# A second pair of projections as seven 2x2 block products per layer, with background steps placed by counted time

## The chip, the cores and the metric

The kernel runs on one core of a Trainium2 chip. The metric is the device time of one execution in microseconds (us), as the median of several runs.

## The reference

Two layers, each of them a pre-norm mixer with a residual, work on x of 256 tokens by 2048 channels, all float32. One wide product gives the inputs of two mixers: `qk`, `v`, `o`, `z_a` of a chunked matrix memory (mLSTM) with eight heads, and `xb`, `z_b` of a gated linear recurrence (RG-LRU). A second product, `w_out`, takes both results back to 2048 channels.

```
u = rms_norm(x, norm_g)
p = u @ w_in
qk, v, o, z_a, ig, fg, xb, z_b = jnp.split(p, SPLIT_AT, axis=-1)
...
h = mlstm_chunkwise(q, k, v, i_pre, log_f)
h = h * jax.nn.sigmoid(o.astype(f32)).reshape(b_, s_, H_A, DV_A)
...
y_a = h.astype(x.dtype) * jax.nn.silu(z_a)
xc = causal_dwconv(xb, lru_conv_w) + lru_conv_b
y_b = rg_lru(xc.astype(f32), w_a, b_a, w_x, b_x, lam).astype(x.dtype) * jax.nn.silu(z_b)
return x + jnp.concatenate([y_a, y_b], axis=-1) @ w_out
```

A last `rms_norm` follows the second layer.

## The kernel before

Each layer is worked off in four groups (0 to 3 in the code, one to four in words) of 512 columns of each of `o`, `qk`, `v`, `xb`, `z` and `zb`. `_sequence` writes the order of the items by hand: the projections of a group, among them the four chunks of `w_out` for the group ahead of it, then the gates. An input projection is four *units* of 1024 KB of weights, and a unit is two *halves*. For a half, `prepare` splits 128x1024 weights into a high part `wH` (ScalarE, a cast) and a low part `wL` (VectorE, a subtraction); TensorE then makes 12 matmuls of 128x512 (`mm_a`, L400): two blocks of the contraction, two halves of the tokens, and three products, high by high, high by low and low by high. Splits stand `AHEAD` = 3 halves ahead of their matmuls, in four buffers each; three buffers `raw` hold units that SP's queue loads.

Everything else (turning to channels, convolutions, scores, gates, scans) is written as generators in the queue `bg`. After a half, `pump` advances them until about `FULL` = 3 us of VectorE work is queued (`st["lag"]`). A generator that has to let time pass yields "wait"; before the change a distance in time is a number of such pumps (`LANDING` = 4, `FAR` = 6, `PACE`). `pump` is called only after plain halves, not after block halves. `require(key)` runs generators until a result is there.

`to_channels` and `swapped` turn a 128x1024 tile from tokens to channels: ScalarE scales it into `tok`, VectorE transposes 32x32 blocks into `blk`, four transfers on SP's queue write `moved` in DRAM, and one on POOL's queue reads it back as `fr`. A later step (`ch<-fr`, `zsg<-fr` or `tok<-fr`) reads `fr`. `ch` is one buffer, shared by the `qk` and `xb` convolutions, the scores `Pt` and `zb`.

One pair of items per layer, `z` of group three and `o` of group four (`PAIR`), is done as a product of 2x2 blocks with seven block products instead of eight: x is cut by 128 tokens and by 1024 channels, the weights by 1024 channels and by the two items' columns. A block product is four *block halves* of 128x1024 weights, each with six matmuls into one PSUM bank `ps_b` (`product`, L1175 to L1177). Products 1 to 4 and 5 to 7 use either x itself or `sums` of its blocks, S1 to S4, that VectorE makes (`block_sums`); on the weights' side plain blocks, or sums that transfers make in DRAM (`weight_sums`): SP copies a block to `w_d`, and accumulating transfers on POOL's queue add others to it. `rawb`, two buffers of 512 KB, holds a block half's weights. Results are added up in `res`. Block halves are spread over the plain halves at the end of the program; the main loop below then emits everything in one order, in which each engine works in its own order.

Of the kernel before, what the change touches and what calls it, by code (L numbers as in the profile page):

```python
# [16 lines left out]
P = 128  # L17
# [11 lines left out]
LANDING = 4  # L29
FAR = 6  # L30
BORDER = 7
BLANKS = 7
PACE = 3, 5
# [9 lines left out]
def _sequence():  # L43


    def units(item):
        return [(item, j) for j in range(_nunits(item))]

    seq = []
    for l in range(DEPTH):  # L50
        for g in range(NG):
            fill = [("out", l, g - 1, c) for c in range(4)] if g > 0 else []
            head = {0: ("o", "qk", "v"), 1: ("qk", "o", "v"), 2: ("qk", "o", "v")}.get(g, ("o", "v", "qk"))
            items = [("in", l, k, g) for k in head]
            at = 2 if g == NG - 1 else 0
            items += fill[0:at] + [("in", l, "xb", g)] + fill[at:4]
            items += [("in", l, "z", g), ("gate", l, g)]
            items.insert(len(items) if g > 0 else -2, ("in", l, "zb", g))
            us = [u for it in items for u in units(it)]
            if l > 0 and g == 0:  # L60
                us[0:8] = [us[i] for i in (0, 4, 1, 5, 2, 6, 3, 7)]
            seq += us
        if l + 1 < DEPTH:
            u = [u for c in range(4) for u in units(("out", l, NG - 1, c))]
            seq += [u[i] for i in (0, 2, 1, 3, 4, 5, 6, 7)]
        else:
            seq += units(("last", l, NG - 1))
    return seq


PAIR = (("z", NG - 2), ("o", NG - 1))


def _blockwise(item):

    return item[0] == "in" and item[2:] in PAIR

# [21 lines left out]
def tile_trunk(ctx, tc, x, xt, par, gw, gb, ws, final_g, out):  # L99
# [30 lines left out]
    st = {"nload": 0, "lag": 0.0, "nprep": 0, "pair": 0, "aux": 0}  # L130
# [165 lines left out]

    def require(key):
        i = 0
        while key not in st:
            i = step(i)  # L300

# [8 lines left out]
    def drain():  # L310
        i = 0
        while bg:
            i = step(i)
# [26 lines left out]
    def load_block(hf):  # L340
        raw = hf["raw"] = wblk.tile([P, 2, 512], F32, tag="rawb", name="rawb")
# [336 lines left out]
    def v_post(l, g, acc):  # L678
        vH = work.tile([P, 2, 2, 258], F32R, tag="sB", name="vH")
# [13 lines left out]
    def qk_post(l, g, acc):  # L693
        bg.append(e_gen(l, g))
        fr = to_channels(l, acc)
        relaxed = 0 < g < NG - 1

        def gen():
            for _ in range(LANDING):
                yield "wait"  # L700
            st["turning"] = True
# [4 lines left out]
            for ct in range(4):  # L706
                conv(ch, qc, ct, O_QKW + 4 * (8 * (ct % 2) + 2 * g + ct // 2), l, None)
                yield 1.45
            if relaxed:
# [17 lines left out]
            while any((k, l, g) not in st for k in ("E", "v", "so")):  # L727
                yield "wait"
            E, em, so, (vH, vL) = st["E", l, g], st["em", l], st["so", l, g], st["v", l, g]
# [21 lines left out]
            tt_(PL, Pt, PH.bitcast(F32), ALU.subtract)  # L751
            yield 1.0
# [36 lines left out]
    def z_post(l, g, acc):  # L789
        require(("hn", l, g))  # L790
        require(("rstd", l))
        rstd = st["rstd", l]
# [10 lines left out]
        def gen():  # L803
# [8 lines left out]
            for _ in range(FAR if g < NG - 1 else LANDING):  # L812
# [6 lines left out]
    def xb_post(l, g, acc):  # L819
        fr = to_channels(l, acc)  # L820

        def gen():
            for _ in range(LANDING):
                yield "wait"
            ch = joined(fr)
            yield 0.3
            xc = work.tile([P, 4, T], F32, tag="c4", name="xc", bufs=2)
            for ct in range(4):
                tix = 4 * g + ct
                conv(ch, xc, ct, O_LW + 4 * tix, l, pars[:, l, O_LB + tix : O_LB + tix + 1])  # L830
                yield 1.45
            while ("scores", l, g) not in st:
# [78 lines left out]
    def zb_post(l, g, acc):  # L911
        ending = (l, g) == (DEPTH - 1, NG - 1)
        fr = to_channels(l, acc, nc.sync if ending else G)

        def gen():
            for _ in range(LANDING - 3 if ending else FAR):
# [3 lines left out]
            while st["turning"]:  # L920
                yield "wait"
            xc, _ = st["xc", l, g]
# [9 lines left out]
            for b in range(2):  # L932
# [3 lines left out]
                yield 0.6  # L936
            if ending:
# [107 lines left out]
    def block_sums(l):  # L1045
# [3 lines left out]
        res = st["res", l] = act.tile([P, 4, 512], F32, tag="res", name="res")  # L1049

        def made(i, key, negated, p, q, pieces=1, after=None):
            to, n = sums[i], 8 // pieces
            for k in range(pieces):
                ks = slice(n * k, n * k + n)
                while after and ("done", l, after, (k + 1) * 4 // pieces - 1) not in st:
# [11 lines left out]
                for f in (difference,  # L1067
# [8 lines left out]
                    if pieces == 1:  # L1076
                        yield "wait"
                        yield "wait"
# [15 lines left out]
        for _ in range(5):  # L1094
            yield "wait"
# [5 lines left out]
    def block_unit(l, r, c, j):  # L1101
        return ws[blocks[("in", l) + PAIR[c], 2 * r + j]]

    wd = [[[dram.tile([P, 2048], F32, name=f"w_d{l}{i}{j}") for j in range(2)] for i in range(2)] for l in range(DEPTH)]

    def weight_sums():

        def moved(l, to, start, r, c, j, h):
            cs = slice(1024 * h, 1024 * h + 1024)
            src = block_unit(l, r, c, j)[:, cs]  # L1110
            while not start and st["n"] - st.get("staged", -9) < 2:
                yield "wait"
            if start:
                order(nc.sync.dma_start(out=wd[l][to][j][:, cs], in_=src), st["ld"])
            else:
                i0 = G.dma_start(out=wd[l][to][j][:, cs], in_=src, accum_op=ALU.add)
                order(i0, st["gq"])
                paced(i0, st["wH"])
            for _ in range(PACE[l]):
                yield "wait"  # L1120

        parts = [(j, h) for j in range(2) for h in range(2)]
        while ("hn", 0, 0) not in st:
            yield "wait"
        for l in range(DEPTH):
            for to, a, b in ((0, (0, 0), (0, 1)), (1, (1, 1), (0, 1))):
                for at in parts:
                    yield from moved(l, to, True, *a, *at)
                    yield from moved(l, to, False, *b, *at)
            for no, a in ((5, (1, 1)), (6, (1, 0))):  # L1130
                for j, h in parts:
                    while ("loaded", l, no, 2 * j + h) not in st:
                        yield "wait"
                    yield from moved(l, 0, False, *a, j, h)

    def block_halves(l):
# [8 lines left out]
        def slot(i):  # L1145
            return st["res", l][:, i]
# [5 lines left out]
        def copied(to):  # L1152
            S.copy(out=slot(to), in_=box["b"])

        def end7():
            add(3, 3)
            g1 = PAIR[1][1]

            def gen():
                while ("lru", l, g1 - 1) not in st:  # L1160
                    yield "wait"
                o_post(l, g1, (slot(2), slot(3)), "neg")
                yield 0
            bg.append(gen())

        def product(A, no, kp, need, end):
            opening = kp == 0 and no in (1, 5, 6)
# [11 lines left out]
            def after():  # L1179
                st["done", l, no, kp] = True  # L1180
                if kp == 3:
                    end()
            need_ = (need, l, kp // 2) if need == "S4" and kp % 2 == 0 else (need, l) if need and kp == 0 else None
            if (no, kp) == (5, 3):
                need_ = ("S2", l)
            return dict(i=kp % 2, mm=f, split=None, paired=False, own=None,
                        before=(lambda: require(need_)) if need_ else None, after=after)

        parts = []
        for no, A, need, end, W in (  # L1190
            (1, plain(0, 0), None, lambda: copied(1), (0, 0)),
            (2, plain(0, 1), None, lambda: copied(0), (1, 0)),
            (5, summed(1), "S1", lambda: add(3, 1), 0),
            (3, summed(1), "S4", lambda: add(2, 1), (1, 1)),
            (6, summed(0), "S2", lambda: add(2, 2), 0),
            (7, summed(1), "S3", end7, 1),
            (4, plain(1, 1), None, lambda: add(1, 1), 0),
        ):
            for kp in range(4):
                src = block_unit(l, *W, kp // 2) if isinstance(W, tuple) else wd[l][W][kp // 2]  # L1200
                hf = product(A, no, kp, need, end)
                hf["from"] = src[:, 1024 * (kp % 2) : 1024 * (kp % 2) + 1024]
                hf["loaded"] = ("loaded", l, no, kp)
                parts.append(hf)
        return parts
# [172 lines left out]
    order_, span = [], {}  # L1378
    for item, j in seq:
        l, what = item[1], item[2:]  # L1380
        if _blockwise(item):
            if what == PAIR[0]:
                span[l] = (span[l][0], len(order_))
            continue
        if (item[0], what) == ("in", ("qk" if l else "o", 1)) and l not in span:
            span[l] = (len(order_), None)
        order_ += [dict(hf, at=(item, j)) for hf in units[item][j]]
    for l in reversed(range(DEPTH)):
        a, b = span[l]
        b += b % 2  # L1390
        order_[b - 1]["then"] = lambda l=l: z_post(l, PAIR[0][1], st["res", l][:, 0:2])
        b -= 6
        parts = block_halves(l)
        gates_ = [n for n, hf in enumerate(order_) if hf.get("at", (("",),))[0][0] == "gate"]
        free = [n for n in range(a, b) if not any(g <= n < g + 8 for g in gates_)]
        for i in reversed(range(len(parts))):
            at = free[(i + 1) * (len(free) - 1) // len(parts)]
            order_[at:at] = [parts[i]]
# [8 lines left out]
    for n, hf in enumerate(order_):  # L1407
# [126 lines left out]
```

## Time and profile before

| | |
|---|---|
| median of three runs | 1483.2 us (1482.11 to 1483.34) |
| the profiled execution's time | 1483.14 us |
| its span, first to last instruction | 1481.3 us |
| granted TensorE clock | 0.998 |
| busy: TensorE, VectorE, ScalarE, GpSimd | 1469.4, 1145.2, 956.4, 108.2 us |
| moved by DMA | 383.43 MB, 259 GB/s in the mean |

PE is TensorE and PEld its weight loads, DVE VectorE, ACT ScalarE, POOL GpSimd, SP the engine whose queue begins most loads. Matmul durations overlap: 390 ns is the mean of one, while they start closer together than that. DMA share is the mean busy share of the core's 16 DMA engines. Most operations of VectorE and ScalarE are issued by one helper and have line L113, so groups are told apart by tile names.

### The profile page before, as it was taken

Reading aid. Unit: us, or ns where it says so; the run is one execution under the profiler, and the core shown is the slowest. Engines: PE = TensorE matmul, PEld = TensorE weight load, DVE = VectorE, ACT = ScalarE, POOL = GpSimd, SP = SyncE. Lnnn points to the kernel's source line nnn. Section 1 sums busy time; section 2 is a strip of 40 time slices with the busy share of each in tenths; the row PEclk is TensorE's granted clock in tenths of the full one; section 3 lists DMA queues with packets and bytes.
Section 4 is the critical chain, followed back from the end, with each engine's and each line's share of the span. In section 5 each row is a group of like instructions: output and inputs, shape, how many; then the busy total and the mean of one; then the engine's idle time right before and its main releaser. Section 6 shows DMA issues by size and latency. Waiting matters only on the chain.

```text
span 1481.3 us, 18779 instructions
## 1 busy us (share of the span) xinstructions
PE 1469.4 (99%) x6782; PEld 1226.8 (83%) x6782; DVE 1145.2 (77%) x1564; ACT 956.4 (65%) x1226; POOL 108.2 (7%) x186
## 2 busy tenths in 40 slices
PE   9999999999999999999999999999999999999997
PEld 7888888888888888788888888888888888888886
DVE  5788888888777676778867889789787776767785
ACT  7666765656665765558565677655667566655675
POOL 0010000100100001000000100000000000010002
PEclk9999999999999999999999999999999999999999
DMA  9866898999978998896786657679799668778783
GB/s 344 323 223 228 264 314 274 291 288 279 313 259 267 281 287 275 270 288 210 279 281 199 234 203 252 235 251 282 234 276 299 214 221 254 250 222 264 238 274 116
DMA packets 104045, 383.43 MB, mean 259 GB/s; under 512 B 11392, under 2 KB 31888, under 8 KB 84496
## 3 DMA queue, kind: packets, MB, share of 16 engines
q1 hardware_dynamic: 87536, 327.41, 63.3%
q0 software_dynamic: 13952, 50.35, 15.6%
q10 hardware_dynamic: 2464, 4.47, 0.8%
q8 instruction: 53, 0.87, 0.2%
q14 instruction: 40, 0.33, 0.1%
HBM read 344.95 MB, written 62.41 MB: 275 GB/s over the span
## 4 chain that ended last, share of the span: by engine, by line
PE 91%; DMA 4%; DVE 2%; ACT 1%; issue 1%; SPq 0%; ACTq 0%; DVEq 0%; POOLq 0%
PE acc L400 78%; PE ps_gt L857 3%; DMA raw<-in_ws_dram 3%; PE ps_b L1175 2%; PE ps_b L1176 2%; PE ps_b L1177 2%; DVE wL L113 1%; PE acc L1273 1%; PE acc L1274 1%; PE acc L1272 1%; DMA xp<-in_xt_dram 1%; DMA pars<-in_par_dram 1%; DMA fr<-moved 0%; PE acc_x L1274 0%; PE acc_x L1273 0%
## 5 line engine op out<-in xcount | busy, mean ns | idle before, releaser
L400 PE MATMUL acc<-wH,x_s 128*128 128x512 f32 x2752 | 860.2, 390 | 0.4 <-ACT wH L113 0.4
L113 DVE TENSOR_TENSOR wL<-raw,wH 128x1024 fp32r<-128x1024 f32 (+1 forms) x500 | 598.2, 1203 | 250.0 <-ACT wH L113 248.1
L113 ACT CAST wH<-raw 128x1024 fp32r<-128x1024 f32 (+1 forms) x500 | 515.1, 1036 | 386.5 <-PE acc L400 307.8
L400 PEld LDWEIGHTS acc<-wH,x_s 128*128 128x128 f32 x2752 | 516.5, 188 | 107.3 <-ACT wH L113 0.8
L400 PE MATMUL acc<-wL,x_s 128*128 128x512 f32 x1376 | 534.3, 389 | 0.0
L400 PEld LDWEIGHTS acc<-wL,x_s 128*128 128x128 f32 x1376 | 258.3, 188 | 52.8
L400 PE MATMUL acc<-wH,ybL 128*128 128x512 f32 x224 | 87.1, 390 | 0.2 <-DVE ybL L964 0.2
L400 PE MATMUL acc<-wH,yaH 128*128 128x512 f32 x224 | 87.2, 389 | 0.0
L400 PE MATMUL acc<-wL,ybH 128*128 128x512 f32 x224 | 87.2, 389 | 0.0
L400 PE MATMUL acc<-wH,ybH 128*128 128x512 f32 x224 | 87.2, 389 | 0.0
L400 PE MATMUL acc<-wH,yaL 128*128 128x512 f32 x224 | 87.2, 389 | 0.0
L400 PE MATMUL acc<-wL,yaH 128*128 128x512 f32 x224 | 87.2, 389 | 0.0
L113 ACT ACT_TABLE_LOAD x61 | 78.3, 1283 | 4.8 <-DVE qc L113 1.4
L113 ACT CAST wH<-rawb 128x1024 fp32r<-128x1024 f32 x56 | 59.0, 1053 | 22.9 <-PE acc L400 10.3
L113 DVE TENSOR_TENSOR wL<-rawb,wH 128x1024 fp32r<-128x1024 f32 x56 | 68.2, 1219 | 3.8 <-ACT wH L113 3.0
L522 POOL DMA_DIRECT2D fr<-moved x34 | 19.0, 559 | 532.7 <-DMA moved<-blk 395.3
L113 DVE STREAM_TRANSPOSE blk<-tok 128x1024 f32<-128x1024 f32 x33 | 40.9, 1240 | 13.3 <-ACT tok L113 13.3
L400 PEld LDWEIGHTS acc<-wH,ybL 128*128 128x128 f32 x224 | 42.0, 188 | 9.3 <-DVE ybL L964 0.6
L400 PEld LDWEIGHTS acc<-wH,yaL 128*128 128x128 f32 x224 | 42.0, 188 | 8.7
L400 PEld LDWEIGHTS acc<-wH,ybH 128*128 128x128 f32 x224 | 42.1, 188 | 8.7
L400 PEld LDWEIGHTS acc<-wL,ybH 128*128 128x128 f32 x224 | 42.0, 188 | 8.6
L400 PEld LDWEIGHTS acc<-wL,yaH 128*128 128x128 f32 x224 | 42.1, 188 | 8.5
(224 smaller groups left out, 1601.5 us busy)
## 6 DMA issues: line engine op xcount, KB each, us to landing
raw<-in_ws_dram SPq DMA_DIRECT2D x152, 1024.0 KB, 6.4
raw<-in_ws_dram SPq DMA_DIRECT2D x190, 512.0 KB, 5.9
fr<-moved POOLq DMA_DIRECT2D x34, 512.0 KB, 6.3
moved<-blk SPq DMA_DIRECT2D x132, 128.0 KB, 2.7
w_d<-in_ws_dram POOLq DMA_DIRECT2D x32, 512.0 KB, 10.0
rawb<-w_d SPq DMA_DIRECT2D x32, 512.0 KB, 6.6
rawb<-in_ws_dram SPq DMA_DIRECT2D x24, 512.0 KB, 6.3
x_d<-stage POOLq DMA_DIRECT2D x24, 512.0 KB, 7.9
```

The costliest lines, as they stand in the source:

```text
L113: ins = f(*a, **k)
L400: st["mm"] = PE.matmul(o, a_[:, kt, P * t : P * t + P], W[:, k], start=b, stop=z)
L522: i0 = back.dma_start(out=fr.rearrange("p a c t i -> p a (c t i)"), in_=moved)
L857: PE.matmul(o, W[:, ib, jl], xs[:, ib, a, :], start=j == 0 and i == 0 and W is Hv and a == 0, stop=i == 1 and W is Lv, skip_group_check=True)
L1175: PE.matmul(box["b"], aH, Hv[:, k], start=opening and k == 0, stop=False, skip_group_check=True)
L1176: PE.matmul(box["b"], aH, Lv[:, k], start=False, stop=False, skip_group_check=True)
L1177: PE.matmul(box["b"], aL, Hv[:, k], start=False, stop=kp == 3 and k == 1, skip_group_check=True)
L1272: PE.matmul(o, yH[:, kt, tsl], Hv[:, k, cs], start=start and k == 0, stop=False)
L1273: PE.matmul(o, yH[:, kt, tsl], Lv[:, k, cs], start=False, stop=False)
L1274: PE.matmul(o, yL[:, kt, tsl], Hv[:, k, cs], start=False, stop=stop and k == 1)
```

## The change

A second pair per layer, `v` and `o` of group three, joins the block products; the other pair becomes `o` and `z` of group four, and `z` of group three is a plain item again. The first pair keeps the order 1, 2 | 5, 3 | 6, 7, 4, the second goes 1, 2 | 6, 7, 4 | 5, 3, where a bar starts a new accumulation in `ps_b`. It uses the S2 and S3 that are there, and VectorE makes S1 and S4 again (S1b, S4b, four pieces each). For the second pair weight sum 0 is copied inside DRAM to a third buffer, by POOL's queue, so that product 5 can be last. `z_post` takes its result from `res` with the sign turned.

```
-PAIR = (("z", NG - 2), ("o", NG - 1))
+PAIRS = (("v", NG - 2), ("o", NG - 2)), (("o", NG - 1), ("z", NG - 1))
...
-            head = {0: ("o", "qk", "v"), 1: ("qk", "o", "v"), 2: ("qk", "o", "v")}.get(g, ("o", "v", "qk"))
-            items = [("in", l, k, g) for k in head]
-            at = 2 if g == NG - 1 else 0
-            items += fill[0:at] + [("in", l, "xb", g)] + fill[at:4]
-            items += [("in", l, "z", g), ("gate", l, g)]
+            head = {0: ("o", "qk", "v", "xb"), 1: ("qk", "o", "v", "xb"), 2: ("qk", "xb", "o", "v")}.get(g, ("qk", "v", "xb"))
+            items = [("in", l, k, g) for k in head] + fill
+            items += [("in", l, k, g) for k in (("o", "z") if g == NG - 1 else ("z",))] + [("gate", l, g)]
...
         yield from made(1, "S1", False, x(1, 1), x(1, 0))
         yield from made(0, "S2", True, s(1), x(0, 0))
-        yield from made(1, "S4", True, s(0), x(0, 1), 2, 5)
-        yield from made(1, "S3", False, x(0, 0), x(1, 0), 4, 3)
+        yield from made(1, "S4", True, s(0), x(0, 1), 2, (0, 5))
+        yield from made(1, "S3", False, x(0, 0), x(1, 0), 4, (0, 3))
+        yield from made(1, "S1b", True, s(0), x(0, 0), 4, (1, 7))
+        yield from made(0, "S4b", True, s(0), x(0, 1), 4, (1, 6))
...
+            for n, at in enumerate(parts):
+                first += [(None, False, copied(0, b(0, 0), at), None), (None, True, added(0, b(0, 1), at), (5, n))]
+                if p == 1:
+                    first += [(None, True, copied(2, lambda j: wd[l][p][0][j], at, G), (5, n)),
+                              (None, True, added(0, b(1, 1), at), (6, n))]
+                else:
+                    late.append((("loaded", l, p, 5, n), True, added(0, b(1, 1), at), (6, n)))
+                other += [(None, False, copied(1, b(1, 1), at), None), (None, True, added(1, b(0, 1), at), (7, n))]
+            late += [(("loaded", l, p, 6, n), True, added(0, b(1, 0), at), (4, n)) for n, at in enumerate(parts)]
```

Distances become times. `st["t"]` counts 2.72 for a plain half and 1.36 for a block half, and a generator waits until it has grown by a number of microseconds. `pump` is called after every half, block halves too. A flag `st["ch"]` lets only one user of the buffer `ch` in. The weight sums begin at half 20 (`SUMS_FROM`) instead of after group one's heads, one job every 6.5 us in the first layer's list and 10 in the second's.

```
-LANDING = 4
-FAR = 6
+LANDING = 10.0
+FAR = 15.0
-PACE = 3, 5
+PACE = 6.5, 10.0
+SUMS_FROM = 20
...
+    def before(t):
+        return st["t"] < t and not st.get("forced")
...
-            for _ in range(LANDING):
-                yield "wait"
-            st["turning"] = True
+            while before(t0 + LANDING) or st.get("ch"):
+                yield "wait"
+            st["turning"] = st["ch"] = True
...
-        if "from" not in hf:
-            pump()
-        st["lag"] = max(0.0, st["lag"] - (1.36 if "from" in hf else 2.72))
+        pump()
+        took = 1.36 if "from" in hf else 2.72
+        st["lag"] = max(0.0, st["lag"] - took)
+        st["t"] += took
```

What this does to the order is seen best on two engines. First ScalarE in layer 0, at `xb` of group four, from the turned tile's `tok` to the copy `ch` that reads what came back. Before:

```order
L113 ACTIVATE tok<-acc,rstd 128x4x4x32 x2
L113 CAST wH<-raw 128x1024 x4
L113 COPY stage<-acc 128x1024
L113 ACT_TABLE_LOAD
L113 ACTIVATE sd<-mv,epst 128x4
L113 CAST wH<-raw 128x1024 x3
L113 COPY ch<-fr 128x1024
```

And now, where `wH<-rawb` is the split of a block half:

```order
L112 ACTIVATE tok<-acc,rstd 128x4x4x32 x2
L112 COPY Pt<-ps_S 128x256
L112 COPY Pt<-ps_S 128x128
L112 CAST wH<-rawb 128x1024
L112 CAST wH<-raw 128x1024 x2
L112 COPY Pt<-ps_S 128x256
L112 COPY Pt<-ps_S 128x128
L112 CAST wH<-rawb 128x1024
L112 CAST PH<-Pt 128x768
L112 CAST wH<-raw 128x1024 x2
L112 COPY ch<-fr 128x1024
```

Between `tok` and `ch` stood seven splits of plain halves; now there are four of plain halves and two of block halves, and the scores' copies `Pt` have moved in between.

Second, POOL's queue in layer 0, around the transfer `nb` of group three's gates. The names w_d_121, 122, 125, 126, 129 and 130 are buffers of weight sums. Before:

```order
L1116 DMA w_d_121<-in_ws_dram 128x1024 x2
L1116 DMA w_d_122<-in_ws_dram 128x1024
L522 DMA fr<-moved 128x1024
L1116 DMA w_d_122<-in_ws_dram 128x1024
L1116 DMA w_d_121<-in_ws_dram 128x1024
L522 DMA fr<-moved 128x1024
L643 DMA nb<-nG_d_119 128x512
L683 MEMSET vH 128x4x2
```

And now, where L1142 is an accumulation and L1133 a copy:

```order
L1142 DMA w_d_122<-in_ws_dram 128x1024 x2
L1133 DMA w_d_129<-w_d_125 128x1024
L1142 DMA w_d_125<-in_ws_dram 128x1024
L529 DMA fr<-moved 128x1024
L1142 DMA w_d_126<-in_ws_dram 128x1024
L1133 DMA w_d_130<-w_d_126 128x1024
L650 DMA nb<-nG_d_119 128x512
L692 MEMSET vH 128x4x2
L529 DMA fr<-moved 128x1024
L1142 DMA w_d_126<-in_ws_dram 128x1024 x2
L1133 DMA w_d_130<-w_d_126 128x1024
```

The second pair's sums have moved in here: an accumulation into w_d_126, a copy that reads what it wrote, and then an accumulation that must not overtake that copy, with `fr` of a turned tile between them.

More of the change, by code (lines that the diff above doesn't have):

```diff
@@ L811, in gen @@
             yield 1.4
-            for _ in range(FAR if g < NG - 1 else LANDING):
+            t0 = st["t"]
+            while before(t0 + (FAR if g < NG - 1 else LANDING)):
                 yield "wait"
@@ L913, in zb_post @@
         fr = to_channels(l, acc, nc.sync if ending else G)
+        t0 = st["t"]
         def gen():
-            for _ in range(LANDING - 3 if ending else FAR):
+            while not ending and before(t0 + FAR):
                 yield "wait"
@@ L1054, in made @@
                 ks = slice(n * k, n * k + n)
-                while after and ("done", l, after, (k + 1) * 4 // pieces - 1) not in st:
+                while after and ("done", l, *after, (k + 1) * 4 // pieces - 1) not in st:
                     yield "wait"
@@ L1145, in slot @@
         def slot(i):
-            return st["res", l][:, i]
+            return st["res", l, p][:, i]
         def add(to, a):
@@ L1179, in after @@
             def after():
-                st["done", l, no, kp] = True
+                st["done", l, p, no, kp] = True
                 if kp == 3:
                     end()
[L1183 to L1198, printed above, removed]
+            needs = [need(kp)] if need else []
@@ L1377, in tile_trunk @@
         units[item] = halves
-    order_, span = [], {}
+    order_, ends = [], {}
     for item, j in seq:
```

200 lines of the change are left out of this document (136 added, 64 removed).

## The prediction

> **What bounds the kernel now.** I read the page first, then the waits of TensorE, the chain of waits, the windows, the groups with shapes kept apart, and last the DMA queues. The page's first lines name the engine that is always busy (PE, TensorE); two of the rows of its waits (waiting, waited for, us in total, times, longest) say that hardly anything holds it up.
>
> ```profile
> span 1481.3 us, 18779 instructions
> PE 1469.4 (99%) x6782; PEld 1226.8 (83%) x6782; DVE 1145.2 (77%) x1564; ACT 956.4 (65%) x1226; POOL 108.2 (7%) x186
> PE ps_S L736 <- DVE Pt L113: 1.4, 1, 1.4
> PE acc L400 <- ACT wH L113: 0.4, 1, 0.4
> ```
>
> A busy TensorE may still run below its peak, so I looked at its pitch. In the chain of waits (start, duration, what), three stretches of 36 plain matmuls with one block half of six between them:
>
> ```profile
> 182.96 8.16 PE acc L400 x36
> 192.48 8.16 PE acc L400 x36
> 202.00 8.16 PE acc L400 x36
> ```
>
> 8.16/36 = 0.2267 us from matmul to matmul, and 192.48 - 182.96 - 8.16 = 1.36 us for the six of the block half, again 0.2267. The matmuls of the new products cost what the old ones cost. The windows (length, busy and count by engine, granted clock, DMA share, GB/s) show where TensorE loses time:
>
> ```profile
> 70.00:700.00 630.00, 628.60 (x2940) 526.88 (x2939) 495.24 (x683) 410.36 (x509) 51.36 (x85) 1.00 0.86 271
> 148.00:630.00 482.00, 480.60 (x2211) 401.30 (x2210) 375.33 (x481) 312.38 (x382) 41.74 (x63) 1.00 0.90 282
> 700.00:1300.00 600.00, 599.81 (x2750) 500.00 (x2749) 477.44 (x632) 387.18 (x489) 36.54 (x68) 1.00 0.76 248
> 592.00:630.00 38.00, 36.60 (x168) 30.31 (x168) 28.80 (x46) 22.58 (x29) 3.65 (x5) 1.00 0.89 272
> 1444.00:1481.00 37.00, 28.91 (x139) 24.23 (x137) 21.41 (x30) 19.47 (x36) 7.72 (x6) 0.94 0.34 120
> ```
>
> Between 70 and 1300 us it loses 1.4 + 0.2 us, the 1.4 in 592 to 630; the last 37 us lose 8.1, on which the change does nothing. So TensorE bounds, and a matmul removed in the middle is worth its pitch, as long as the cover holds. The cover is thinnest in layer 0, where the DMA share is 0.90.
>
> **The change, part by part.** *Matmuls.* Two plain items of 4 units, each of 24 matmuls, are 192; seven products of 4 block halves, each of 6, are 168. That is 24 less in a layer, 48 in all, at 0.2267 us: **-10.9 us**, all of it on the path, since nothing else does. The Trainium skill (TensorE: Matmul & The Clock Gate, section Back-to-back issue gap) gives for 512 columns about 216 ns for a single one and about 131 ns sustained; by these the term would be -10.4 or -6.3. The trace disagrees with both at 226.7 ns, and it decides.
>
> *Splits and sums on VectorE and ScalarE.* The rows of before, per shape:
>
> ```profile
> L113 DVE TENSOR_TENSOR wL<-rawb,wH 128x1024 fp32r<-128x1024 f32 x56 | 68.2, 1219 | 3.8 <-ACT wH L113 3.0
> L113 ACT CAST wH<-rawb 128x1024 fp32r<-128x1024 f32 x56 | 59.0, 1053 | 22.9 <-PE acc L400 10.3 <-PE ps_b L1177 10.2 <-issue 1.1
> L113 DVE TENSOR_TENSOR res<-res,ps_b 128x512 f32<-128x512 f32 x10 | 6.8, 680 | 0.0
> L113 DVE TENSOR_TENSOR sum_t<-sum_t,x_s 128x256 f32<-128x256 f32 x16 | 6.7, 418 | 0.3
> L113 DVE CAST sums<-sum_t 128x256 fp32r<-128x256 f32 x8 | 2.3, 288 | 0.2
> L113 ACT COPY res<-ps_b 128x512 f32<-128x512 f32 x4 | 2.4, 588 | 1.6 <-PE ps_b L1177 1.6
> ```
>
> A block half needs the split of a plain half for half its matmuls. Instead of 16 plain halves there are 28 block halves, in two layers 24 more: 24 x 1.219 = 29.3 us on VectorE and 24 x 1.053 = 25.3 on ScalarE. S1b and S4b are 16 pieces of four operations near 0.418 and a cast of 0.288, 1.96 us each, 31.4 us; ten more additions into `res` are 6.8. VectorE gets 67.5 us: 1145.2 + 67.5 = 1212.7, 82% of 1472. ScalarE gets 25.3, four copies of 0.588 and two more table loads, some 30 us: 986, 67%. Both stay below TensorE, and I cost them at nothing. What hides them is the lead: splits stand three halves ahead of their matmuls, 8.2 us of plain halves, and only some 5.4 where block halves stand between. Without it each of them would cost TensorE its whole duration.
>
> *Transfers.* The queues, with packets, MB and their share of 16 engines' span, and the issues with KB and us to landing:
>
> ```profile
> q1 hardware_dynamic: 87536, 327.41, 63.3%
> q0 software_dynamic: 13952, 50.35, 15.6%
> raw<-in_ws_dram SPq DMA_DIRECT2D x152, 1024.0 KB, 6.4
> fr<-moved POOLq DMA_DIRECT2D x34, 512.0 KB, 6.3
> w_d<-in_ws_dram POOLq DMA_DIRECT2D x32, 512.0 KB, 10.0
> x_d<-stage POOLq DMA_DIRECT2D x24, 512.0 KB, 7.9
> w_d<-in_ws_dram SPq DMA_DIRECT2D x16, 512.0 KB, 8.1
> ```
>
> On q1 a plain MB costs 0.633 x 1481.3 / 327.41 = 2.86 us of all 16 engines, 512 KB (0.524 MB) 1.50. On q0 there are 0.156 x 1481.3 = 231 us; the 34 `fr` and some 3 MB of broadcasts take 21 MB x 2.86 = 60 at the plain price, so the 56 accumulating transfers took (231 - 60)/56 = 3.05 us each, an estimate. Added are 56 `rawb` loads for 16 `raw` of 1024 KB (24 pieces of 512 KB, 36 us), 16 plain copies on SP (24), eight on POOL (12) and 32 accumulations (98): 170 us, from 63.3 + 15.6 = 78.9% of the span (1169 us) to (1169 + 170)/1472 = 91%. The copy from one `w_d` to another isn't in the trace; it lies between the copies on SP (8.1 us to landing) and the accumulations (10.0), and I take the copy's price, since nothing is added in it.
>
> Half of the added work, 85 us, is layer 0's. In 148 to 630 that makes 0.90 x 482 = 434, plus 85 x 482/630 = 65, so 499 us of work in 477 us: 1.05. From two bounds: nothing if the engines have that much room, 22 us if 1.00 is their end. Six-microsecond windows of before show what they can do at the utmost:
>
> ```profile
> 36.00:42.00 6.00, 6.00 (x28) 4.95 (x28) 3.50 (x5) 4.40 (x10) 0.00 (x0) 1.00 1.05 418
> 270.00:276.00 6.00, 6.00 (x33) 5.14 (x32) 4.97 (x13) 4.22 (x6) 0.00 (x0) 1.00 1.05 304
> ```
>
> The share ends at 1.05, once with 418 GB/s and once with 304, so the busy share holds waiting as well as work, and a full share alone stalled nothing at 270. I therefore take late single transfers instead of a bound. What one costs stands in the chain near 592, and in ScalarE's waits after 60 us (total, times, longest):
>
> ```profile
> 585.53 7.20 DMA fr<-moved
> 592.76 1.06 ACT ch L113
> 599.66 11.85 DMA raw<-in_ws_dram
> 611.60 1.06 ACT wH L113
> ACT wH L113 <- PE acc L400: 317.6, 223, 5.4
> ACT wH L113 <- DMA raw<-in_ws_dram: 26.6, 11, 4.6
> ```
>
> Eleven loads came late and ten of them cost TensorE nothing; the worst, 11.85 us to landing and 4.6 us of ScalarE's time, cost the 1.4. In layer 0 the share goes from 0.90 to about 1: I take three such stalls instead of one, **+2.8 us**.
>
> *Landing counted in time, queues, the lock.* Turned blocks are now awaited 10 us of TensorE time after their start, where four pumped halves took more as soon as block halves stood between. At the place shown on ScalarE, `tok` to `ch` goes from seven plain halves (19.0 us) to four plain and two block halves (13.6). The trace has `tok` at 624.15 and the `fr` transfer issued at 631.75:
>
> ```profile
> 624.15 1.27 ACT L113 ACTIVATE tok<-acc,rstd 128x512 f32<-128x512 f32 x2 [1.62 <-PE acc L400]
> 631.75 0.56 POOL L522 DMA_DIRECT2D fr<-moved  x1 [30.04 <-DMA moved<-blk]
> ```
>
> 7.6 + 6.3 to land is 13.9 us, so ScalarE, with the `wH` of the coming halves queued behind it, waits 0.3 us there. On POOL, `fr` now stands behind accumulations, and behind copies that wait for the accumulation ahead of them; with 10.0 us to landing against a pace of 6.5, `fr` may be 3.5 us later. 0.3 + 3.5 = 3.8 us is less than the 4.6 which cost 1.4, so each such place lies between nothing and 1.4; they are in the 2.8. The `ch` lock keeps an engine from standing before a buffer still in use; its gain is at most the 1.4 of `ps_S`. SP begins 16 more copies and 40 more transfers of 512 KB, ahead of loads; by its rows that is half a microsecond or less each, and SP waits for buffers far longer:
>
> ```profile
> L1114 SPq DMA_DIRECT2D w_d<-in_ws_dram x16: 497/509/1004, 53.8 to 612.5; - x16
> SPq L336 <- DVE wL L113: 468.3, 116, 8.1
> ```
>
> So I cost that at nothing. No load on SP should wait for an accumulation: counted over the order, the last one stands at least 40 us of TensorE time ahead of the load that reads it.
>
> Sum, against the profiled execution's 1483.14 (the median is 1483.2): 1483.1 - 10.9 + 2.8 = **1475.0 us**.
>
> **The rivals.** *Stalls eat the gain.* Each of the eight groups loses 1.4 us to a late `fr` or load, the old stall included: 8 x 1.4 - 1.4 = 9.8, 1482.0 us. For it: the distances shrink in all groups, and POOL's queue is longer. Against it: ScalarE idles 317.6 us for TensorE's buffers, so there is lead. *DMA becomes the bound in layer 0.* The accumulations, at 3.05 us each, take turns with the weight loads, and 22 us of excess over a share of 1.00 come back as late loads: 1483.1 - 10.9 + 22 = 1494 us. It decides as soon as the share in layer 0's middle stays at 1.00 or over and TensorE loses several us in each window. For it: 1.05 of demand; against it: the two windows above. The Trainium skill (DMA: Bandwidth & Descriptors, section Issuing engines are not separate DMA queues) says that transfers begun by different engines run on the same 16 DMA engines and interleave; by that rule an accumulation on POOL's queue delays the loads on SP's; the trace agrees at 599.66, where a load took 11.85 us. *The whole gain and the old stall with it.* The lock and the evener pump also take the 1.4 away: 1483.1 - 10.9 - 1.4 = 1470.8.
>
> **How the numbers follow.** A measurement of this kernel can tell about 0.2%, 3 us. Forecast (1471.5 to 1480) 0.62, whole gain 0.10, gain eaten 0.16, DMA bound 0.12. Faster: forecast and whole gain, 0.72; the same, 1480.2 to 1486.2, 0.16; slower, 0.12. The range goes from the whole gain, 1470.5, to 1486.0, past the eaten gain; it leaves out the DMA bound and little else.
>
> **What would show it.** Right: 48 matmuls fewer with the pitch still 0.2267 us, TensorE's idle time between 70 and 1300 us at 3 to 6 us, VectorE near 82%, DMA near 91%. Wrong: waits of TensorE for `wH` that begin with `raw` landing after over 12 us (DMA bound), waits behind `ch` (landing too short), POOL waiting for `w_d` with `fr` behind it, or a pitch that changed.

## The result, and the profile after

The change made the kernel slower: 1492.93 us in the median of eleven runs (1487.17 to 1502.6), beside 1483.58 us for the kernel before (eleven runs, 1481.24 to 1485.22). The ratio is 1.0072, with a 95% interval of 1.0048 to 1.0097. The runs of the changed kernel spread over 1%, those of before over 0.3%. The profiled execution took 1500.83 us and lies at the upper end of that spread, so what is read from it is larger than in a median run.

The page of the changed kernel begins like this (span; busy time, share and count by engine), and has these two DMA queues (packets, MB, share of 16 engines' span):

```profile
span 1499.1 us, 19073 instructions
PE 1470.4 (98%) x6734; PEld 1223.4 (82%) x6734; DVE 1194.8 (80%) x1678; ACT 981.2 (65%) x1256; POOL 142.0 (9%) x226
...
q1 hardware_dynamic: 95600, 348.39, 65.5%
q0 software_dynamic: 19712, 71.33, 21.9%
```

TensorE does have 48 matmuls fewer (6734 for 6782), and yet is busy as long as before. VectorE and ScalarE stay below the 1212.7 and 986 us that the prediction worked out, with room left. The two queues take 87.4%.

The windows say where the time went. First long ones, then four of 8 us (length, busy and count by engine, granted clock, DMA share, GB/s):

```profile
70.00:700.00 630.00, 617.79 (x2852) 516.32 (x2851) 510.72 (x729) 413.53 (x514) 68.61 (x104) 0.99 0.95 300
148.00:630.00 482.00, 473.02 (x2149) 393.75 (x2148) 392.21 (x519) 315.48 (x386) 48.97 (x75) 0.99 0.96 304
700.00:1300.00 600.00, 596.11 (x2733) 495.92 (x2733) 482.96 (x648) 393.25 (x494) 54.19 (x89) 1.00 0.87 278
1300.00:1445.00 145.00, 142.62 (x659) 117.86 (x657) 119.02 (x179) 98.03 (x124) 8.07 (x13) 1.00 0.77 256
...
410.00:418.00 8.00, 3.25 (x14) 2.12 (x12) 3.90 (x8) 5.49 (x9) 0.83 (x1) 0.99 0.70 185
418.00:426.00 8.00, 7.86 (x28) 6.37 (x29) 8.00 (x13) 4.68 (x8) 0.00 (x0) 0.79 0.95 283
450.00:458.00 8.00, 4.66 (x12) 3.79 (x13) 7.83 (x13) 4.72 (x10) 0.89 (x1) 0.63 0.93 229
794.00:802.00 8.00, 5.05 (x19) 3.72 (x18) 4.69 (x13) 7.95 (x10) 0.00 (x0) 0.89 0.65 222
```

Between 70 and 1300 us TensorE now loses 12.2 + 3.9 = 16.1 us, where it lost 1.6, and 2.4 more up to 1445 us. The loss sits in a few places. In the window from 418 on TensorE is busy for 7.86 us and starts only 28 matmuls, where 8 us at 0.2267 hold 35: the granted clock of this window is 0.79, and each matmul takes longer. The prediction did not have that at all.

The waits of TensorE, and of ScalarE for transfers after 60 us (waiting, waited for, us in total, times, longest):

```profile
PE ps_S L748 <- DVE Pt L112: 4.1, 1, 4.1
PE acc L407 <- DVE wL L112: 3.5, 3, 1.8
PE ps_gt L874 <- ACT gate L879: 3.2, 1, 3.2
PE acc L407 <- ACT wH L112: 3.1, 1, 3.1
PE acc L407 <- ACT so L112: 3.0, 1, 3.0
...
ACT ch L112 <- DMA fr<-moved: 24.9, 9, 6.7
ACT wH L112 <- DMA raw<-in_ws_dram: 30.7, 13, 5.9
```

TensorE waits for splits, `Pt`, a gate, `so`; behind them on ScalarE stands a transfer that landed late. `ch` waited for `fr` once, 0.3 us, after 60 us of before, and now nine times; the loads `raw` went only from 26.6 to 30.7 us in all. The stall at 412 us, in the timelines of ScalarE, SP, GpSimd and TensorE (start, duration, what, and in brackets the idle time ahead and what ended it):

```profile
388.31 1.27 ACT L112 ACTIVATE tok<-acc,rstd 128x512 f32<-128x512 f32 x2 [0.61 <-PE acc L407]
390.89 3.92 SPq L528 DMA_DIRECT2D moved<-blk  x4
403.66 0.60 POOL L529 DMA_DIRECT2D fr<-moved  x1 [2.24 <-DMA moved<-blk]
412.48 1.04 ACT L112 COPY ch<-fr 128x1024 f32<-128x1024 f32 x1 [6.68 <-DMA fr<-moved]
415.85 0.50 PE L407 MATMUL acc<-wH,x_s 128*128 128x512 f32 x1 [3.10 <-ACT wH L112]
418.14 0.79 PE L407 MATMUL acc<-wL,x_s 128*128 128x512 f32 x1 [1.79 <-DVE wL L112]
```

And the issues between 385 and 413 us (KB each, us to landing):

```profile
moved<-blk SPq DMA_DIRECT2D x4, 128.0 KB, 9.1
fr<-moved POOLq DMA_DIRECT2D x1, 512.0 KB, 8.8
```

`tok` was begun at 388.31. The four `moved` transfers took 9.1 us to land in the median, where the page of before has 2.7, and `fr` 8.8 instead of 6.3. GpSimd had nothing left to do when it waited 2.24 us for `moved`, so its queue did not hold `fr` back here. From `tok` to `ch` 24.2 us passed, while the new distance counts on 10; the order leaves five splits of plain halves and three of block halves between them, 17.7 us at this place (the 13.6 of the prediction belong to `xb` of group four). ScalarE stood 6.68 us, the casts behind it were late, and TensorE lost 3.10 + 1.79 us. The other places have the same form: until 442.70 `ch` waits for `fr` 5.09 us, then `Pt` is late; until 670 and 676 two casts wait for `raw` 3.75 and 4.23 us, then the gates are late; until 792 a cast waits for `raw` 5.94 us, then `so` is late; until 1437 `tok` waits for `fr` 4.49 us, and TensorE loses 0.72 + 1.15 us at 1444.

### The profile page after: what moved, and what is told of

Same layout as the page of the kernel before. It is cut to its first block, busy times and chain, and to the rows that moved or that the text cites. A ratio compares the mean times of both kernels' runs of the same rounds, so it can differ in the third digit from the quotient of the medians.

```text
span 1499.1 us, 19073 instructions
## 1 busy us (share of the span) xinstructions
PE 1470.4 (98%) x6734; PEld 1223.4 (82%) x6734; DVE 1194.8 (80%) x1678; ACT 981.2 (65%) x1256; POOL 142.0 (9%) x226
## 5 line engine op out<-in xcount | busy, mean ns | idle before, releaser
L407 PE MATMUL acc<-wH,x_s 128*128 128x512 f32 x2496 | 786.1, 390 | 6.0 <-ACT wH L112 3.1
L407 PEld LDWEIGHTS acc<-wH,x_s 128*128 128x128 f32 x2496 | 469.7, 188 | 104.8 <-ACT wH L112 4.2
L407 PE MATMUL acc<-wL,x_s 128*128 128x512 f32 x1248 | 486.3, 391 | 3.5 <-DVE wL L112 3.5
L112 DVE TENSOR_TENSOR wL<-rawb,wH 128x1024 fp32r<-128x1024 f32 x112 | 136.4, 1218 | 38.7 <-ACT wH L112 38.6
L112 ACT CAST wH<-rawb 128x1024 fp32r<-128x1024 f32 x112 | 117.6, 1050 | 71.3 <-PE acc L407 47.2
L407 PE MATMUL acc<-wH,yaL 128*128 128x512 f32 x224 | 87.6, 391 | 0.0
L407 PE MATMUL acc<-wH,ybH 128*128 128x512 f32 x224 | 87.4, 390 | 0.0
L1142 POOL DMA_DIRECT2D w_d<-in_ws_dram x64 | 55.0, 859 | 298.9 <-ACT wH L112 183.4
L112 DVE SCALAR_TENSOR_TENSOR qc<-ch,pars,qc 128x255 f32<-128x255 f32 (+2 forms) x96 | 42.3, 475 | 11.8 <-ACT qc L112 11.5
L1230 PE MATMUL ps_b<-wL,sums 128*128 128x512 f32 x128 | 50.0, 390 | 0.1
L1229 PE MATMUL ps_b<-wH,sums 128*128 128x512 f32 x128 | 50.1, 391 | 0.0
L1231 PE MATMUL ps_b<-wH,sums 128*128 128x512 f32 x128 | 49.9, 389 | 0.0
L407 PEld LDWEIGHTS acc<-wH,yaH 128*128 128x128 f32 x224 | 42.5, 190 | 8.9
```

The lines of the kernel that those rows point to most:

```text
L112: ins = f(*a, **k)
L407: st["mm"] = PE.matmul(o, a_[:, kt, P * t : P * t + P], W[:, k], start=b, stop=z)
L1142: i0 = G.dma_start(out=wd[l][p][to][j][:, cs], in_=src(j)[:, cs], accum_op=ALU.add)
L1229: PE.matmul(box["b"], aH, Hv[:, k], start=opening and k == 0, stop=False, skip_group_check=True)
L1230: PE.matmul(box["b"], aH, Lv[:, k], start=False, stop=False, skip_group_check=True)
L1231: PE.matmul(box["b"], aL, Hv[:, k], start=False, stop=kp == 3 and k == 1, skip_group_check=True)
```

## The experiments

The theory after this look: the weight sums' transfers lengthen the landing of everything that is awaited, and the shorter distances leave no room for it. The rivals: the distances alone; the place behind accumulations on GpSimd's queue; VectorE and ScalarE; the layout in the second layer.

**Longer distances.** Edit on the changed kernel:

```
-LANDING = 10.0
-FAR = 15.0
+LANDING = 16.0
+FAR = 21.0
```

> The changed kernel with the awaited times longer: 16 instead of 10 us (LANDING) and 21 instead of 15 (FAR), about what the order of before had. If the steps that read a turned block simply stand too early (theory landing), ScalarE's waits at ch<-fr, 24.9 us in the changed kernel, shrink below 5, TensorE's stalls at 410 to 458 us go, and the time falls to 1476 to 1482 us. If the DMA engines are short of room (theory DMA load), loads of raw stay late, the stalls move elsewhere, and the time stays at 1488 to 1500.

Measured: 1487.11 us (12 runs), before 1484.68 beside it, ratio 1.0014 (1.0001 to 1.0026). ScalarE's wait for `fr` at `ch` falls from 24.9 to 15.2 us. The time lies between the two ranges, and the wait at `ch` did not fall below 5: the stall at 410 is still there, with gaps of 2.39 and 1.80 us on TensorE. Some 6 us of the loss hung on the distance; the gain of the matmuls is still gone.

**No weight sums, with both distances.** The copies and accumulations are left out, and the block products load plain blocks in their place, so that the result lacks the weights' sums; all matmuls, splits and loads stay. The edit of the accumulations is shown; the copies return in the same way.

```
 def f():
     j, cs = at
-    i0 = G.dma_start(out=wd[l][p][to][j][:, cs], in_=src(j)[:, cs], accum_op=ALU.add)
-    order(i0, st["gq"])
-    paced(i0, st["wH"])
+    return
...
-src = block_unit(l, p, *W, kp // 2) if isinstance(W, tuple) else wd[l][p][W][kp // 2]
+src = block_unit(l, p, *W, kp // 2) if isinstance(W, tuple) else block_unit(l, p, 0, 0, kp // 2)
```

> The changed kernel without the transfers that make the weight sums: all copies and accumulations into w_d are left out, and the products that should read sums load a plain block of the same size, so the sums of the weights are missing from the result. Awaited times as in the changed kernel. Theory DMA load: the DMA share falls by some 20 points in layer 0, the late transfers go, and the time falls to 1472 to 1477 us. Theory landing: turned blocks still land 14 us after tok against 13.6 to 16.3 in the order, half of ScalarE's 24.9 us at ch<-fr stay, and the time is 1480 to 1488.

> Both at once: no transfers for the weight sums (the same part of the result is missing) and the longer awaited times 16 and 21 us. Both theories expect the floor here, 1483.5 less 10.9 of matmuls, 1471 to 1474 us; a higher time would be a cause that neither names, for instance VectorE's 67 us of added work.

Measured: 1478.83 us with 10 and 15 (ratio 0.9953, 0.9939 to 0.9968), between the two ranges, and 1471.42 with 16 and 21 (0.9911, 0.9897 to 0.9925), the expected floor. Of the latter the page's software queue, and then its first layer in the windows:

```profile
q0 software_dynamic: 9344, 33.58, 9.0%
```

```profile
70.00:700.00 630.00, 630.00 (x2948) 528.25 (x2947) 529.90 (x748) 424.25 (x526) 30.89 (x62) 1.00 0.76 251
```

TensorE loses nothing in the first layer, though VectorE and ScalarE do all their added work. Against the 1484.68 of before this is 13.3 us less; the matmuls' 10.9 and the old stall's 1.4 make 12.3, and the interval (11.1 to 15.3) holds that. Set in a square, the sums' transfers cost 1492.93 - 1478.83 = 14.1 us with the short distances and 1487.11 - 1471.42 = 15.7 with the long ones; the short distances cost 5.8 with the transfers and 7.4 without. By the ratios to the kernel before, measured beside each, they are 17.7 and 15.3 for the transfers, 8.6 and 6.2 for the distances; the interval of the changed kernel alone is 3.6 us to either side. Within that the two costs add up; neither is the other's condition.

**Copies instead of accumulations**, with 16 and 21 us. The order of all queues stays, and the packets and MB of the software queue too.

```
-i0 = G.dma_start(out=wd[l][p][to][j][:, cs], in_=src(j)[:, cs], accum_op=ALU.add)
+i0 = G.dma_start(out=wd[l][p][to][j][:, cs], in_=src(j)[:, cs])
```

> As the run with 16 and 21 us, but every accumulating transfer of weights is a plain copy of the same block into the same place (the sums are not added, all else is in place, bytes written and the order of the queues too). Theory (the engines' time that an accumulation takes beyond a copy is what crowds the loads, 80 accumulations here by about 1.5 us): the DMA share of 70 to 700 us falls from 0.96 to about 0.85 and the time from 1487 to 1474 to 1478 us. Rival (the place of fr behind them on GpSimd's queue, or the 40 more loads, whatever an accumulation costs): 1484 us or more.

Measured: 1477.75 us (ratio 0.9955, 0.9943 to 0.9967). Its software queue and the first layer's windows, and then the same two of the kernel with accumulations and 16 and 21 us:

```profile
q0 software_dynamic: 19712, 71.33, 16.3%
```

```profile
70.00:700.00 630.00, 627.63 (x2930) 524.58 (x2929) 525.85 (x746) 422.18 (x524) 55.07 (x105) 1.00 0.90 307
```

```profile
q0 software_dynamic: 19712, 71.33, 22.2%
```

```profile
70.00:700.00 630.00, 621.17 (x2872) 519.25 (x2871) 515.44 (x732) 414.37 (x515) 68.94 (x104) 0.99 0.96 303
```

The same transfers in the same places, only without the addition, give 9.4 of the 15.7 us back; the first layer's share falls from 0.96 to 0.90, and TensorE loses 2.4 us there instead of 8.8. What is left, 1477.75 - 1471.42 = 6.3 us, goes with their bytes and their place, those of SP's copies included. The order of GpSimd's queue alone is therefore not the cause, since `fr` stands behind as many transfers in both. Whether the addition acts through the 16 engines' time, or through the later landing that the next transfer of that queue waits for, this run does not separate. The prices come out of the queue: 0.163 x 1474.9 - 0.090 x 1468.6 = 108 us for 72 copies, 1.50 each, and (0.222 x 1485.2 - 0.163 x 1474.9)/64 = 1.40 us more for the addition: 2.90 us of 16 engines for 512 KB accumulated.

**One layer at a time**, with 16 and 21 us: the second pair only in the second layer, or only in the first. In the other layer `v` and `o` of group three are the one pair.

```
-    return item[0] == "in" and any(item[2:] in pair for pair in PAIRS)
+    return item[0] == "in" and any(item[2:] in pair for pair in PAIRS[: 1 + (item[1] in SECOND)])
...
-        queues = [jobs(l, p) for l in range(DEPTH) for p in range(2)]
+        queues = [jobs(l, p) if p == 0 or l in SECOND else deque() for l in range(DEPTH) for p in range(2)]
```

> The second pair in the second layer only, with 16 and 21 us; the first layer has one pair (v and o of group three). Theory (the transfers cost where the DMA share is near 1, and that is in the first layer): half of the matmul gain, 5.4 us, stays: 1477 to 1480 us, DMA share of 148 to 630 us near 0.90. Rival (each added accumulation costs the same anywhere): about half of what both cost, 1484 us.

> The second pair in the first layer only, with 16 and 21 us. Theory (costs lie where the share is near 1): 1486 to 1491 us, slower than before though it has 24 matmuls less, the share of 148 to 630 us at 0.97. Rival (costs alike in both layers): 1484 us, as with the second layer alone.

Measured: 1477.77 us with the second layer alone (ratio 0.9963, 0.995 to 0.9975), 1496.18 with the first alone (1.0076, 1.0063 to 1.0089), beside 1484.1 of before. Windows of the former, then of the latter:

```profile
70.00:700.00 630.00, 627.24 (x2931) 525.21 (x2931) 493.61 (x679) 407.19 (x506) 61.15 (x99) 1.00 0.92 288
700.00:1300.00 600.00, 598.52 (x2740) 497.94 (x2739) 489.06 (x654) 394.35 (x499) 44.65 (x74) 1.00 0.81 262
```

```profile
70.00:700.00 630.00, 619.84 (x2865) 516.81 (x2864) 513.15 (x730) 411.53 (x511) 67.77 (x104) 0.99 0.95 300
...
1445.00:1510.00 65.00, 42.19 (x183) 34.08 (x181) 27.93 (x36) 24.95 (x41) 7.72 (x6) 0.90 0.33 113
```

Here lies the difference that the square could not show: 24 matmuls fewer are worth about their pitch in the second layer, and cost in the first, where TensorE loses 10.2 us between 70 and 700. The second layer's version beats both kernels. The first layer's came out 5 us beyond what was expected; its end has lost more too (53.6 - 42.2 = 11.4 us idle from 1445 on, at a clock of 0.90, where before had 8.4). A late end comes without a second pair too, as the next runs show; why it is late here was not tried.

**Counting in time in the kernel before**, one pair per layer, with 10 and 15 and then 16 and 21 us, paces of 8.16 and 13.6 us, the pump after every half, the lock. As in the changed kernel, the last turned block's own wait (`LANDING - 3` pumps) and some waits of the block sums go too; a part of the edit:

```
-LANDING = 4
-FAR = 6
+LANDING = 10.0
+FAR = 15.0
...
-            for _ in range(LANDING):
+            while before(t0 + LANDING) or st["ch"]:
...
-        if "from" not in hf:
-            pump()
+        pump()
+        st["t"] += took
```

> The kernel before, with one pair per layer as it was, but with the distances counted in time (10 and 15 us), pumping after every half, the flag on ch and the pace of the sums in time (8.16 and 13.6 us). It does one part of the change alone, with no transfer added. Theory landing: slower than before, 1486 to 1492 us, with ScalarE waiting at ch<-fr for over 10 us in all. Theory DMA load: within 2 us of before, 1482 to 1485.5.

> The kernel before, one pair per layer, with time counting, the pump after every half and the lock, as in the run with 10 and 15 us, but with 16 and 21 us. Theory (the 10 us are too short, and that is all that counting in time costs): the 6 us of that run go away, 1483 to 1485 us, waits of ScalarE for ch under 3 us. Rival (the lock, or the pump after block halves, shifts the work for the worse): it stays near 1490 us.

Measured: 1490.75 us (ratio 1.0039, 1.0026 to 1.0052) and 1491.48 (1.0043, 1.0028 to 1.0059). ScalarE's wait for `fr` between 60 and 1440 us and the windows with the short distances, then a window and some steps of the chain at the end (start, duration, what) with the long ones:

```profile
ACT ch L113 <- DMA fr<-moved: 17.0, 6, 7.3
```

```profile
70.00:700.00 630.00, 628.24 (x2928) 525.88 (x2927) 490.82 (x681) 407.88 (x507) 55.20 (x85) 1.00 0.86 272
700.00:1300.00 600.00, 596.89 (x2731) 496.09 (x2730) 470.57 (x627) 383.46 (x486) 40.20 (x68) 1.00 0.76 244
```

```profile
700.00:1300.00 600.00, 599.16 (x2745) 499.05 (x2744) 475.21 (x631) 386.03 (x488) 39.22 (x68) 1.00 0.76 246
```

```profile
1436.61 5.15 DMA moved<-blk
...
1442.26 7.97 DMA raw<-in_ws_dram
...
1454.36 0.80 PE acc L1287
```

With 10 us both the time and the wait at `ch` came as the theory of the distance said; with 16 the 6 us did not go away, and the trace says why only in part. With 10 us the middle loses 1.8 + 3.1 = 4.9 us, behind `ch` in the first layer (7.3 us until 402), in the second in part behind `nb`, for which VectorE waits 3.9 us until 834; with 16 it loses 0.4 + 0.8, so in the middle the distance was all of it. But then the end is late: the last turned block and a load of 7.97 us hold up the last product at 1454. Which of the edits moved the end was not tried.

**The second layer's sums later**, with 16 and 21 us. They begin at half 270, about 650 us, at a pace of 6.5 us, once with the second pair only in the second layer and once with all pairs.

```
-PACE = 6.5, 10.0
+PACE = 6.5, 6.5
+HOLD = 270
...
-ready = [i for i, q in enumerate(queues) if q and (q[0][0] is None or q[0][0] in st)]
+ready = [i for i, q in enumerate(queues) if q and (i < 2 or st["n"] >= HOLD) and (q[0][0] is None or q[0][0] in st)]
```

> The second pair in the second layer only, as in the run before, but the second layer's weight sums start at half 270, about 650 us, with a pace of 6.5 us instead of from about 400 us on with 10. Theory (a sum's transfer costs where the share is near 1): the 1.2 us that 70 to 700 us lost more than before come back: 1475.5 to 1477.5 us. Rival (only the number of transfers counts): 1478 us again, with the stalls now between 700 and 1000 us.

> The change with 16 and 21 us, both layers with two pairs, and the second layer's weight sums not before half 270 (about 650 us), pace 6.5 us. Theory: the first layer's own sums make most of the loss, so only the stall at 672 to 688 us goes: 1483 to 1486 us. Rival (the second layer's sums in the last third of the first are what crowds it): 1478 us or less.

Measured: 1493.31 us (ratio 1.0063, 1.0047 to 1.0078) and 1492.46 (1.0051, 1.0039 to 1.0063). Theory and rival both failed in the number. Of the first of the two, windows, then GpSimd, VectorE, ScalarE and TensorE near 830 us; after that GpSimd of the version without the delay:

```profile
70.00:700.00 630.00, 630.00 (x2947) 528.19 (x2946) 497.70 (x685) 410.25 (x510) 43.48 (x77) 1.00 0.82 260
700.00:1300.00 600.00, 589.85 (x2681) 488.93 (x2680) 474.92 (x637) 385.29 (x487) 56.03 (x96) 0.99 0.92 288
```

```profile
823.64 0.81 POOL L1146 DMA_DIRECT2D w_d<-in_ws_dram  x1 [12.87 <-ACT scs L114]
824.16 0.83 POOL L624 DMA_DIRECT2D nG_d<-scs  x1
832.12 0.60 POOL L652 DMA_DIRECT2D nb<-nG_d  x1 [7.13 <-DMA nG_d<-scs]
838.36 1.01 DVE L114 TENSOR_SCALAR E<-nb,at 128x256 f32<-128x256 f32 x4 [8.07 <-DMA nb<-nG_d]
839.40 0.84 ACT L114 ACTIVATE E<-E 128x768 f32<-128x768 f32 x1 [6.51 <-DVE E L114]
842.62 0.80 PE L409 MATMUL acc<-wH,x_s 128*128 128x512 f32 x1 [5.99 <-ACT wH L114]
```

```profile
824.27 0.52 POOL L623 DMA_DIRECT2D nG_d<-scs  x1 [25.89 <-DVE scs L113]
826.15 0.56 POOL L651 DMA_DIRECT2D nb<-nG_d  x1 [1.36 <-DMA nG_d<-scs]
```

The first layer now loses nothing at a share of 0.82. The second now has the share of 0.92 that the first had without the delay, and loses 10.2 us, where the first lost 2.8. The difference is what stands there: `nG_d`, begun half a microsecond behind an accumulation on the same queue, was waited for 7.13 us instead of 1.36 (it landed at 831.83, the accumulation at 831.40), and `nb` came late. VectorE stood 8.07 us, ScalarE 6.51 us at the next step of `E` with the `wH` of the coming halves behind it, and TensorE 5.99. The version with all pairs has the same stall, 6.44 us at 841. Here the place on GpSimd's queue did count. The share by itself does not set the price; what is awaited beside the transfers, and with how much room, does.

**Stalls by themselves.** In the kernel before the cast of six halves is repeated:

```
+            for _ in range(CASTS.get(st["n"], 0)):
+                S.copy(out=H[:, o], in_=r[:, o])
             st["wH"] = S.copy(out=H[:, o], in_=r[:, o])
```

> The kernel before, in which the cast of six halves is repeated 8, 10, 12, 14, 17 and 20 times more on ScalarE (the same values written again), some 80 us apart, from about 800 us on: stalls of TensorE of several sizes with nothing else changed. Theory (after a stall of some us the granted clock falls for about 4 us, so that a stall costs itself and some 2 us more): the matmuls after the long ones stand at 0.43 us, and after stalls under about 2 us at 0.227; six stalls of together about 25 us cost about 35. Rival (the low clock in after came from the load on the whole chip, the DMA engines too): the pitch stays at 0.227 after every stall.

Measured: 1572.45 us in one run, 87.6 more than the 1484.84 of before beside it. TensorE's rows at the old stall, at the first of the six and after it:

```profile
616.07 0.39 PE L739 MATMUL ps_S<-qks 128*128 128x256 f32 x1 [2.05 <-DVE Pt L114]
...
616.64 0.40 PE L403 MATMUL acc<-wL,x_s 128*128 128x512 f32 x1
...
853.83 1.74 PE L403 MATMUL acc<-wH,x_s 128*128 128x512 f32 x2 [5.79 <-ACT wH L114]
...
857.48 0.63 PE L403 MATMUL acc<-wL,x_s 128*128 128x512 f32 x1
...
858.76 0.63 PE L403 MATMUL acc<-wL,x_s 128*128 128x512 f32 x1
```

The stalls were longer than planned (5.79 to 18.10 us; TensorE's waits for splits are 69.6 + 2.8 = 72.4 us in all), and the kernel lost 15.2 us more than they last, 2.5 us for each of the six. Counted from the starts of the same matmuls in both traces it is 2.0 us for the longest to 3.4 for the shortest, so the price does not grow with the stall. After the stall of 2.05 us a matmul lasts 0.40 us as ever; after that of 5.79 it lasts 0.63, and from 857.48 to 858.76 three are started, a pitch of 0.43. A low clock needs nothing but the stall; the rival falls.

## Why the prediction was wrong

- *Matmuls, -10.9 us.* Right: 48 fewer, the pitch unchanged outside the stretches after stalls, and without the sums' transfers the kernel gains all of it.
- *Splits and sums at nothing.* Right: 630.00 of 630 us in the run without the transfers. VectorE got 49.6 us of work where 67.5 were worked out, ScalarE 24.8 where it was some 30.
- *The transfers' amount.* Right: an accumulation measured 2.90 us for the estimate of 3.05, a copy 1.50 for 1.50, and the queues took 0.874 x 1499.1 = 1310 us where 1339 were worked out.
- *From amount to time.* This is the step that failed: "I take three such stalls instead of one, **+2.8 us**." The transfers' term measured 14 to 18 us. The stalls were not three of 1.4 us but four places of 3.0 to 4.9 us between 70 and 1300 and one of 1.9 at 1444; the price of a late transfer had been taken from the one that before happened to show.
- *The shorter distance*, "so each such place lies between nothing and 1.4". It cost 6 to 9 us more. At the place that the working looked at, now 622 to 637 us, `ch` waited 1.51 us and TensorE lost nothing; the loss came at 412 and 442. The working took 7.6 us from `tok` to `fr` out of before, when `moved` landed in 2.7 us, and lengthened `fr` only; at 412 us `moved` took 9.1. A leg of the path was left at its old duration while the engines under it were filled.
- *What a stall costs.* Missing from the sum. In the profiled execution five places are followed by a low clock (410, 450, 682, 794, 1445). Counted from the starts, the matmuls there took 9.2 us longer than at 0.2267. -10.9 for the matmuls, +14.5 idle from 70 to 1300, +2.4 to 1445, and 9.2 give +15.2; the difference of the two profiled executions is 1500.83 - 1483.14 = 17.7, and the other 2.5 us lie in starts a little later than the pitch, whose cause stays open. The Trainium skill (TensorE: Matmul & The Clock Gate, section HAM oscillation — how this bites in real kernels) says that idle gaps beyond about 3.4 us set the array back to half its clock. The runs agree for 5.79 us and for 2.05, but show the low clock also after shorter gaps: one of 2.95 us at 796 in the changed kernel, two of 2.39 and 1.80 us close together with 16 and 21 us, and two of 0.98 and 0.76 us at 403 in the kernel before with 10 and 15 us (granted clock 0.51 from 406 to 409). A stall of 1.4 us, which alone had no such price in the kernel before, was the wrong unit.
- *The rivals.* "DMA becomes the bound in layer 0" came nearest in time (1494), and its place was right, but the nearness is luck. One of its signs showed in part: two loads ahead of the stall at 680 took 12.6 and 13.4 us to land. Its condition did not hold: the share of 148 to 630 us was 0.96, and TensorE lost time in a few places, not several us in each window. The way was that of "Stalls eat the gain", late `fr` and loads in single places, at about four times its price for each when the low clock is counted in.

## What to carry to other kernels

A kernel whose bound is hidden by leads is priced by its awaited transfers: for each, add up every leg from producer to reader at the landing times that the loaded queues will have, and set that sum against the distance in the order. Work for idle DMA engines goes where awaited transfers have room; here the same 24 matmuls saved were a gain of 6 us in the second layer and a loss in the first, and with the sums begun later the second layer's version lost 8.5 us as well. Price a stall as its length plus what the clock takes after it.

## What the runs showed of the hardware

- After stalls of TensorE of 5.8 to 18.1 us the matmuls of 512 columns stand at 0.43 us instead of 0.227 until 4 to 7 us after it went on, which costs 2.0 to 3.4 us each time; after one of 2.05 us they do not. Below some 3 us length alone did not decide: two gaps of 0.98 and 0.76 us were followed by a granted clock of 0.51, two of 1.18 and 0.76 us at 768 in the run with the delayed sums in the second layer alone by 1.00.
- An accumulating transfer of 512 KB inside DRAM takes 2.90 us of the 16 DMA engines, a plain copy of the same queue 1.50.
- From the kernel before to the changed one the small transfers lengthened most: the median to landing of the 128 KB `moved` went from 2.7 to 4.4 us, that of a 1024 KB load from 6.4 to 7.5.
